# Seven products instead of eight for the convolution's output projection, a fifth early pair, and the memory values computed earlier

## The chip, the cores and the metric

The kernel runs on one core of one Trainium2 chip. The metric is the device time of one execution in microseconds (us); lower is better. The core has a matrix engine (TensorE, PE in the profile), VectorE (DVE), ScalarE (ACT), GpSimd (POOL) and SyncE (SP), whose queue issues all DMA transfers of this kernel. SBUF is the working memory, PSUM holds the sums of matrix products, and each engine works through its own list of instructions in order.

## The reference

A two-layer trunk on x of 1024 tokens by 1024 channels, with 256 memory tokens, in float32. Layer 0 mixes by attention and retention, layer 1 by a gated convolution, and each layer then adds a cross-attention into the memory. What matters here is layer 1:

```python
def conv_mixer(xn, w_in, conv_w, conv_b, w_out):
    gb, gc, u, gate = jnp.split(xn @ w_in, 4, axis=-1)
    z = gc * u
    zp = jnp.pad(z, ((0, 0), (C_CONV - 1, 0), (0, 0)))
    conv = conv_b
    for j in range(C_CONV):
        conv = conv + zp[:, j:j + s] * conv_w[j]
    y = gb * conv * jax.nn.silu(gate)
    return y @ w_out
...
x = x + conv_mixer(rmsnorm(x, o_norm[j]), ...)
x = x + memory_cross_attention(rmsnorm(x, c_norm[i]), rmsnorm(mem, c_mem_norm[i]), ...)
```

`w_in` is 1024 x 4096, `w_out` 1024 x 1024. In the cross-attention keys and values are products of the normed memory with 1024 x 1024 matrices, and queries one of the normed x.

## The kernel before, in words

**Precision.** Every large product is made from float32 data split into a high part (a copy rounded to the matmul's type, by ScalarE) and a low part (data minus high part, by VectorE): `split` (L204) for data, `Weights.whole` (L83) and `Weights.factor` (L92) for weights. `mm3` (L185) then issues three matmuls for each block of 128 x 128 weights and up to 512 columns: high x high (L189), high x low (L190), low x high (L191).

**Layout.** Activations lie channels by tokens: 8 tiles of 128 channels x 1024 tokens. `dense` (L193) makes one tile of outputs from one weight tile (128 x 1024) in two halves of 512 tokens, each of 8 blocks, 24 matmuls.

**Weights.** `Weights` takes an ordered list of weight tiles (L1065). Each is loaded by SP (L76) into one of two raw buffers, split into pages (three high buffers, three low ones) as soon as a page is free, and taken in order by the products. `prepare` (L112) works ahead as far as pages reach.

**Seven products.** `strassen` (L629) makes a pair of output tiles from 4 weight blocks (A11, A12, A21, A22; 128 outputs x 512 inputs each) and 4 activation blocks (B11 to B22; 512 channels x 512 tokens) with seven products instead of eight (Winograd's form): weights A11, A12, S1 to S4, A22 against B11, B21, T1, T2, T3, B22, T4. A product is 4 blocks x 3 = 12 matmuls. The sums S1 to S4 (L99 to L102) are made from the raw weights, by GpSimd, for the first pair by VectorE. The factors T1 to T4 are made by `right_factors` (L564) from the normed x, on VectorE, in an order fixed by `issue_after`; T2 has two buffers of its own. Before, only the convolution's input projection (`conv_in`, L707: 16 pairs, 112 products) is made like this. `times` (L670) turns products into y or z: z multiplies two of the four parts (L683 on GpSimd, L689 on VectorE), y is a gate's silu times another part.

**Early pairs.** The first two products of a pair need only B11 and B21, which come from the first half of the tokens. `conv_start` (L693) issues these two for the first EARLY = 4 pairs, so that PE has work while the norm of the second half and T1 to T4 are made.

**The stages around the change.** `out_proj_halves` (L301) is layer 0's last output projection, first half of the tokens, then the second. Between the tiles of the first half `keys_out` (L790) makes layer 1's memory keys and stores them to DRAM (24 matmuls of 256 columns per tile). Then follow `conv_start`, `conv_in`, and `out_proj` (L281), the convolution's output projection with whole products on the split y: per tile it loads the residual x (L287), adds it (L291), squares the result on ScalarE (L247), sums squares on GpSimd (L249), and stores x. Between its first four tiles `mem_v` (L823) makes the memory values (8 steps of 12 matmuls). `gained` (L915) splits the new x tiles times a gain for the queries, and `cross` (L882) follows.

**Order.** The program is traced in the order of the code, and a list scheduler with a simulated timeline sets each engine's order from readiness and program order. PSUM has 8 buffers of 512 columns: "d" 3, "sc" 2, "a" 3. SBUF buffers go by tag (L165): xh and xl 8 each, r 8, e 4, T 5, v 4, t 5.

Of the kernel before, what the change touches and what calls it, by code (L numbers as in the profile page):

```python
# [22 lines left out]
P = 128  # L23
D = 1024
# [7 lines left out]
EARLY = 4  # L32
# [8 lines left out]
class Weights:  # L41
# [5 lines left out]
    FACTORS = ("A11", "A12", "S1", "S2", "S3", "S4", "A22")  # L47
    LATER = FACTORS[2:]

    def __init__(self, tc, pool, sums, order):  # L50
# [10 lines left out]
        for _, f in self.units:  # L61
            self.tags.append(("whi", "wlo") if f is None else (("whi", "wlo")[pages % 2],))
            pages += f is not None
        self.next = 0
        self.used = 0
        self.factors = {}

    def load(self, i):
        if i >= len(self.order) or i in self.raw:
            return  # L70
        entry = self.order[i]
        tiles = []
        for k, ap in enumerate(entry[:2] if isinstance(entry, tuple) else (entry,)):
            t = self.pool.tile([P, D], F32, tag="wraw", bufs=WRAW, name=f"wraw{i}_{k}")
            for c in halves(i == 0):
                self.nc.sync.dma_start(t[:, c], ap[:, c])  # L76
            tiles.append(t)
# [14 lines left out]
    def factor(self, u, i, f):  # L92
        if f == self.order[i][2][0]:
# [9 lines left out]
            self.factors = F  # L103
        t = self.page(self.tags[u][0], f"wf{u}")
        src, hi, lo = self.factors[f], t[:, :H], t[:, H:]
# [3 lines left out]
        if f == self.order[i][2][-1]:  # L109
            self.raw.pop(i)  # L110

    def prepare(self, upto=None):  # L112

        while self.next < len(self.units) and (upto is None or self.next <= upto):
# [5 lines left out]
            self.load(i)  # L120
            if f is None:
# [7 lines left out]
    def take(self):  # L129
        u = self.used  # L130
# [5 lines left out]
class Trunk:  # L136
# [144 lines left out]
    def out_proj(self, ys, x_old, x_new, between=iter(())):  # L281
# [17 lines left out]
        return xs, old  # L299

# [263 lines left out]
    def right_factors(self, x, gain, h, out):  # L564
# [6 lines left out]
             for i in range(2) for j in range(2)}  # L571
        def normed(f):
            for k in range(4):
# [4 lines left out]
        def split(f, src):  # L578
            for k in range(4):
                if f in ("T2", "T1"):  # L580
# [3 lines left out]
                else:  # L584
                    tag = {"B11": "xh", "B21": "xh", "T3": "xl", "B22": "xl", "T4": "Tn"[k // 2]}[f]
                    t = self.buf(tag, f, dt=F32R)
# [12 lines left out]
        T2 = [t[:, i, :] for t in (self.buf("T", "T2", (P, 2, H)) for _ in range(2)) for i in range(2)]  # L599
# [23 lines left out]
        with ExitStack() as behind:  # L623
            for make in (t1, t2, t3, lambda: split("B22", B["B22"]), t4):
                last = make()
                behind.enter_context(self.tc.issue_after(last.ins))
                behind.enter_context(self.tc.issue_after(self.last_cast.ins))

    def strassen(self, B, out, early=False):  # L629
# [3 lines left out]
        def product(ps, f, first, weights=None):  # L633
            ah, al = weights or self.w.take()
            with self.tc.issue_after(self.last_mm.ins) if early == 0 and early is not False else ExitStack():
# [4 lines left out]
        def kept(ps):  # L640
            t = self.buf("t", "kept", (P, H))
            self.nc.scalar.copy(t, ps)
            return t

        a, b = self.ps("sc" if early is False or early < 2 else "d"), self.ps("d")
        if early is False:
            product(a, "B11", True)
            p1 = kept(a)
            product(b, "B21", True)
        else:  # L650
            wh, wl = self.w.take()
            product(a, "B11", True, (wh[:, :H], wl[:, :H]))
            p1 = kept(a)
            product(b, "B21", True, (wh[:, H:], wl[:, H:]))
        out(0, 0, b, p1)
        yield
# [7 lines left out]
        product(c, "B22", False)  # L664
        out(0, 1, c, u2)
        product(a, "T4", False)
        out(1, 0, a, None)
        yield

    def times(self, B, d, act=None, early=False):  # L670
# [3 lines left out]
        kept = []  # L674

        def out(i, j, ps, more):
            c = d[:, half[j]]
            if i == 0:
# [3 lines left out]
                if j:  # L682
                    nc.gpsimd.tensor_tensor(c, c, kept[0], op=ALU.mult)  # L683
# [7 lines left out]
        return self.strassen(B, out, early)  # L691

    def conv_start(self, B):  # L693
# [13 lines left out]
    def conv_in(self, B):  # L707
# [3 lines left out]
        def pair(i):  # L711
            if i < EARLY:
                d, steps = self.started[i]
            else:
                d = self.buf("v", "z" if i % 2 else "y1")
                steps = self.times(B, d, None if i % 2 else AF.Silu)
# [7 lines left out]
        for m in range(KT):  # L724
# [3 lines left out]
            nc.scalar.activation(cv, z, AF.Identity, bias=w[3], scale=w[2])  # L728
            nc.vector.scalar_tensor_tensor(cv[:, 1:], z[:, : S - 1], w[1], cv[:, 1:],
                                           ALU.mult, ALU.add)  # L730
# [347 lines left out]
```

## Time and profile before

| | |
|---|---|
| time, median of 3 runs | 1484.37 us (1483.30 to 1485.54) |
| profiled execution | 1482.23 us, its span 1480.1 us, mean clock of TensorE 0.994 |
| PE busy | 1438.2 us (97%), 7218 instructions |
| DVE / ACT / POOL busy | 878.1 / 634.8 / 322.7 us |
| conv_start and conv_in | 801.3 to 1133.4 us of the span |
| convolution's output projection | 1133.4 to about 1246 us |
| read from / written to memory | 122.80 / 25.17 MB |

Times inside the profile are microseconds from the span's start. "PE busy" counts matmuls that overlap in a pipeline, so a busy PE is not PE at its peak: the rate of matmuls in a stretch tells more. A timeline row has the start, the length, the engine, the line, the operation with output <- input, the count, and in brackets the idle time before it and what ended that. A row of waits reads: engine and line that waited, the releaser, us in total, times, longest. In the rows by stretch each engine has its busy time and (x) its instructions, followed by the clock granted to TensorE (1.00 is full), the DMA engines' busy share and GB/s.

### The profile page before, as it was taken

The numbers are of one execution on the slowest core, as the hardware profiler recorded it, in microseconds if no ns is written. First come the engines' busy times: TensorE is split into PE (matmuls) and PEld (weight loads), VectorE is DVE, ScalarE is ACT, GpSimd is POOL, SyncE is SP. The second block draws the span as 40 slices with busy tenths as digits, with TensorE's granted clock in tenths as the row PEclk, the third lists the DMA queues.
The fourth block names the chain that finished last, engine by engine and source line by source line (L and its number), as shares of the span: only waits on it lengthen the run. The fifth ranks groups of instructions, "written<-read, shape, count | busy, mean of one in ns | idle before, by whom it ended". The sixth has DMA issues, their size and how long they took to land.

```text
span 1480.1 us, 18711 instructions
## 1 busy us (share of the span) xinstructions
PE 1438.2 (97%) x7218; PEld 1215.4 (82%) x7218; DVE 878.1 (59%) x1289; ACT 634.8 (43%) x1139; POOL 322.7 (22%) x201
## 2 busy tenths in 40 slices
PE   8999999999899999999999799999999999999996
PEld 6888888888788888888888578888888888888996
DVE  7656765656674346446456967666665337446555
ACT  6434662334463344335344533333352325335554
POOL 2300103233311110000213455333340220000233
PEclk9999999999999999999999899999999999999999
DMA  6410114221365421013764121111125532111364
GB/s 216 149 65 29 58 30 142 61 79 48 119 224 170 151 92 43 29 42 129 226 201 143 42 86 58 57 57 57 58 86 213 186 128 72 39 33 40 127 210 152
DMA packets 51625, 153.38 MB, mean 104 GB/s; under 512 B 6352, under 2 KB 14672, under 8 KB 51024
## 3 DMA queue, kind: packets, MB, share of 16 engines
q1 hardware_dynamic: 51536, 152.19, 31.7%
q8 instruction: 57, 0.93, 0.3%
q14 instruction: 32, 0.26, 0.1%
HBM read 122.80 MB, written 25.17 MB: 100 GB/s over the span
## 4 chain that ended last, share of the span: by engine, by line
PE 79%; DVE 8%; DMA 5%; POOL 3%; issue 2%; ACT 2%; SPq 0%; DVEq 0%; POOLq 0%; ACTq 0%
PE psd L191 17%; PE psd L189 17%; PE psd L190 17%; PE pssc L191 5%; PE pssc L189 5%; PE pssc L190 5%; PE psa L190 4%; PE psa L189 4%; PE psa L191 4%; DMA swap<-bk 1%; PE pssc L367 1%; DMA swap<-bq 1%; PE psa L397 1%; PE psa L871 1%; POOL bk L432 1%
## 5 line engine op out<-in xcount | busy, mean ns | idle before, releaser
L189 PE MATMUL psd<-xh,whi 128*128 128x512 f32 (+2 forms) x1096 | 414.2, 381 | 7.7 <-ACT whi L87 7.3
L190 PE MATMUL psd<-xl,whi 128*128 128x512 f32 (+2 forms) x1096 | 414.7, 379 | 0.0
L191 PE MATMUL psd<-xh,wlo 128*128 128x512 f32 (+2 forms) x1096 | 414.3, 379 | 0.2 <-DVE wlo L88 0.2
L189 PEld LDWEIGHTS psd<-xh,whi 128*128 128x128 f32 x1096 | 206.4, 188 | 43.2 <-ACT whi L87 7.8
L191 PEld LDWEIGHTS psd<-xh,wlo 128*128 128x128 f32 x1096 | 206.3, 188 | 35.6 <-DVE wlo L88 0.7
L190 PEld LDWEIGHTS psd<-xl,whi 128*128 128x128 f32 x1096 | 206.5, 188 | 34.0
L87 ACT CAST whi<-wraw 128x1024 fp32r<-128x1024 f32 (+1 forms) x135 | 140.8, 1045 | 213.9 <-PE psd L190 131.0
L88 DVE TENSOR_TENSOR wlo<-wraw,whi 128x1024 fp32r<-128x1024 f32 (+1 forms) x135 | 169.1, 1254 | 71.1 <-ACT whi L87 71.0
L249 POOL TENSOR_TENSOR ssq<-ssq,xold 128x512 f32<-128x512 f32 (+2 forms) x54 | 84.6, 1567 | 574.5 <-ACT xold L247 503.0
L106 ACT CAST wf<-ws 128x512 fp32r<-128x512 f32 x64 | 39.7, 622 | 95.2 <-PE pssc L191 27.7
L291 DVE TENSOR_TENSOR xnew<-psd,xold 128x512 f32<-128x512 f32 x32 | 21.9, 690 | 96.4 <-PE psd L191 93.1
L189 PE MATMUL pssc<-T,wf 128*128 128x512 f32 x168 | 67.1, 399 | 6.6 <-ACT T L205 4.2
L190 PE MATMUL pssc<-T,wf 128*128 128x512 f32 x168 | 67.2, 400 | 1.9 <-DVE T L206 1.9
L191 PE MATMUL pssc<-T,wf 128*128 128x512 f32 x168 | 66.9, 398 | 0.0
L247 ACT ACTIVATE xold<-xnew 128x512 f32<-128x512 f32 (+2 forms) x63 | 36.5, 580 | 66.9 <-DVE xnew L291 37.1
L107 DVE TENSOR_TENSOR wf<-ws,wf 128x512 fp32r<-128x512 f32 x64 | 51.8, 811 | 20.7 <-ACT wf L106 19.6
L107 DVE TENSOR_TENSOR wf<-wraw,wf 128x512 fp32r<-128x512 f32 x40 | 55.1, 1393 | 5.0 <-ACT wf L106 5.0
L205 ACT CAST Th<-psa 128x512 fp32r<-128x512 f32 (+1 forms) x62 | 34.3, 588 | 54.2 <-PE psa L871 29.5
L206 DVE TENSOR_TENSOR Tl<-psa,Th 128x512 fp32r<-128x512 f32 (+1 forms) x62 | 41.7, 686 | 21.4 <-ACT Th L205 21.1
L278 DVE TENSOR_TENSOR q<-psd,R 128x512 f32<-128x512 f32 x32 | 22.1, 691 | 53.8 <-PE psd L191 53.8
L99 POOL TENSOR_TENSOR ws<-wraw 128x512 f32<-128x512 f32 x15 | 32.0, 2131 | 90.5 <-DMA wraw<-w_o_in 90.5
L189 PE MATMUL psd<-y,whi 128*128 128x512 f32 x128 | 50.0, 391 | 0.0
(324 smaller groups left out, 2949.4 us busy)
## 6 DMA issues: line engine op xcount, KB each, us to landing
wraw<-w_o SPq DMA_DIRECT2D x40, 512.0 KB, 4.2
wraw<-w_o_in SPq DMA_DIRECT2D x36, 512.0 KB, 3.6
wraw<-w_e_in SPq DMA_DIRECT2D x25, 512.0 KB, 3.6
wraw<-w_k SPq DMA_DIRECT2D x16, 512.0 KB, 3.9
xold<-x SPq DMA_DIRECT2D x16, 512.0 KB, 5.1
wraw<-w_v SPq DMA_DIRECT2D x16, 512.0 KB, 3.8
x<-xnew SPq DMA_DIRECT2D x16, 512.0 KB, 2.6
wraw<-w_q SPq DMA_DIRECT2D x16, 512.0 KB, 3.5
```

Of the source, the lines that this page charges most:

```text
L87: self.nc.scalar.copy(hi[:, c], raw[:, c])
L88: self.nc.vector.tensor_tensor(lo[:, c], raw[:, c], hi[:, c].bitcast(F32), op=ALU.subtract)
L99: tt(F["S1"], F["A21"], F["A22"], op=ALU.add)
L106: self.nc.scalar.copy(hi, src)
L107: self.nc.vector.tensor_tensor(lo, src, hi.bitcast(F32), op=ALU.subtract)
L189: mm(o, ah, bh, start=first, stop=False, skip_group_check=more)
L190: mm(o, ah, bl, start=False, stop=False, skip_group_check=more)
L191: self.last_mm = mm(o, al, bh, start=False, stop=last, skip_group_check=more)
L205: self.last_cast = self.nc.scalar.copy(hi, src)
L206: return (eng or self.nc.vector).tensor_tensor(lo, src, hi.bitcast(F32), op=ALU.subtract)
L247: nc.scalar.activation(sq, x, AF.Square)
L249: eng.tensor_tensor(self.ssq[:, a:b], self.ssq[:, a:b], sq, op=ALU.add)
```

## The change

- `EARLY` becomes 5, and the fifth early pair's output lies in a T buffer, its accumulator in an "a" buffer.
- The weight sums of the first pair of the input projection are an entry of their own ("sums") ahead of the early pages: its two tiles are loaded, the four sums made, and the raw buffers freed; A22 is loaded again as a half page later.
- The order of the products within a pair becomes B11, T1, B21, T2, T3, B22, T4. The last pair of each projection has the last two swapped, and the convolution's last tile is made in halves.
- T2 takes T1's place instead of two T buffers. The last multiplication of y and z moves from GpSimd to VectorE.
- The convolution's output projection becomes `out_proj_pairs`: four pairs of seven products. Its factors come from `right_factors` without gain and norm. The residual is loaded for a pair when its first product is kept, and VectorE adds it as it keeps a product (`keep`; in `times` it is a copy on ScalarE). Weight sums there are VectorE's. The squares' sums go from GpSimd to VectorE. The first product (B11) of the first OUT_EARLY = 3 pairs is issued ahead.
- Layer 1's memory values are made together with the keys between the first half's tiles of `out_proj_halves`, stored to DRAM (`values_out`) and loaded back behind the projection (`values_in`). `mem_v` is left to layer 0, and a second load of the normed memory goes.
- The first query products of `cross` use the "sc" buffers.

The core of the diff:

```diff
-EARLY = 4
+EARLY, OUT_EARLY = 5, 3
...
-    FACTORS = ("A11", "A12", "S1", "S2", "S3", "S4", "A22")
-    LATER = FACTORS[2:]
+    FACTORS = ("A11", "S1", "A12", "S2", "S3", "S4", "A22")
+    LATER = ("S1", "S2", "S3", "S4", "A22")
+    SWAPPED = ("A11", "S1", "A12", "S2", "S3", "A22", "S4")
...
+        if f == "sums":
+            self.summed = {j for j, e in enumerate(self.order)
+                           if j > i and isinstance(e, tuple) and e[0] is self.order[i][0]}
+            self.raw.pop(i)
+            return
...
+    def out_proj_pairs(self, B, x_old, x_new, early):
...
+        def pair(n):
+            old, new = [], []
+
+            def fetch():
+                for i in range(2):
+                    old.append(self.buf("v", "xold"))
+                    nc.sync.dma_start(old[i], x_old[2 * n + i])
+                new.extend(self.buf("r", "xnew") for _ in range(2))
+                xs[2 * n : 2 * n + 2] = new
+
+            def keep(i, j, ps):
+                t = self.buf("t", "kept", (P, H))
+                if not old:
+                    fetch()
+                nc.vector.tensor_tensor(t, ps, old[i][:, half[j]], op=ALU.add)
+                return t
+
+            def out(i, j, ps, more):
+                c = half[j]
+                x, sq = new[i][:, c], self.buf("t", "sq", (P, H))
+                nc.vector.tensor_tensor(x, ps, old[i][:, c] if more is None else more, op=ALU.add)
+                end = 2 * n + 2 == KT and i != j
+                self.squares(j in seen, x, sq, c.start, c.stop, None if end else nc.vector)
...
+                nc.sync.dma_start(x_new[2 * n + i][:, c], x)
+            return self.strassen(B, out, keep, None, n if n < early else False,
+                                 2 * n + 2 == KT)
+
+        started = []
+        for n in range(early):
+            started.append(pair(n))
+            next(started[n])
+        for n in range(KT // 2):
+            for _ in started[n] if n < early else pair(n):
+                pass
...
+        if gain is None:
+            tags = {"B11": "xh", "T1": "xh", "T3": "xl", "B22": "xl", "T4": "Tv"}
+            inside = ("B21", "T2")
...
-        T2 = [t[:, i, :] for t in (self.buf("T", "T2", (P, 2, H)) for _ in range(2)) for i in range(2)]
+        T2 = T1
...
-        a, b = self.ps("sc" if early is False or early < 2 else "d"), self.ps("d")
-        if early is False:
+        a = self.ps("sc" if (early or apart or 0) < 2 else "a" if early == 4 else "d")
+        if early is None:
             product(a, "B11", True)
-            p1 = kept(a)
-            product(b, "B21", True)
+            if apart is not False:
+                yield
+            p1 = keep(0, 0, a)
...
         c = self.ps("a")
         product(c, "T1", True)
-        p5 = kept(c)
+        p5 = keep(1, 1, c)
+        if early is None:
+            b = self.ps("d")
+            product(b, "B21", True)
+            out(0, 0, b, p1)
         product(a, "T2", False)
-        u2 = kept(a)
+        u2 = keep(0, 1, a)
         product(a, "T3", False)
         out(1, 1, a, p5)
...
+        for block in (c21, c12) if swapped else (c12, c21):
+            block()
...
-                    nc.gpsimd.tensor_tensor(c, c, kept[0], op=ALU.mult)
+                    nc.vector.tensor_tensor(c, c, kept[0], op=ALU.mult)
...
-                d = self.buf("v", "z" if i % 2 else "y1")
+                d = self.buf("v" if i < 4 else "T", "z" if i % 2 else "y1")
...
+    def values_out(self, mem):
+        self.vd = self.dp.tile([2, P, 2, D], F32, name="vd")
+        for ch in range(2):
+            ps = [self.ps("sc"), self.ps("sc")]
+            for kp in range(4):
+                self.value_step(mem, ps, kp)
+                if kp == 3:
+                    c = slice(ch * H, ch * H + H)
+                    for kk in range(2):
+                        hi, lo = (self.buf("t", "V", (P, H), F32R) for _ in range(2))
+                        self.split(hi, lo, ps[kk])
+                        nc.sync.dma_start(self.vd[0, :, kk, c], hi.bitcast(F32))
+                        nc.sync.dma_start(self.vd[1, :, kk, c], lo.bitcast(F32))
+                yield
...
-        self.out_proj_halves(ys, xd[0], xd[1], self.keys_out(self.mem_parts(1, "T")), after)
+        mem = self.mem_parts(1, "T")
+        both = (None for _ in zip(self.keys_out(mem), self.values_out(mem)))
+        self.out_proj_halves(ys, xd[0], xd[1], both, after)
         ys = self.conv_in(B)
...
-        ys = [self.split_k(y) for y in ys]
-        x, rest = self.out_proj(ys, xd[1], xd[2], kv)
+        B = {}
+        for h in range(2):
+            self.right_factors(ys, None, h, B)
+        x, rest = self.out_proj_pairs(B, xd[1], xd[2], OUT_EARLY)
+        K, V = self.keys_in(), self.values_in()
         xs = self.gained(x, 2)
...
+    for m, w in enumerate(tiles("w_o0")):
+        order += [w] + mem1[2 * m : 2 * m + 2]
+    order += tiles("w_o0") + [(*o_in[:2], ("sums",), True)] + o_in[: 2 * EARLY : 2]
+    order += [(*o_in[:2], W.LATER[:4]), o_in[1][:, H:]]
+    for i in range(2, len(o_in), 2):
+        last = i + 2 == len(o_in)
+        order.append((o_in[i], o_in[i + 1],
+                      W.LATER if i < 2 * EARLY else W.SWAPPED if last else W.FACTORS)
+                     + (True,) * last)
+    order += [w[:, :H] for w in o_out[: 2 * OUT_EARLY : 2]]
+    for i in range(0, len(o_out), 2):
+        last = i + 2 == len(o_out)
+        order.append((o_out[i], o_out[i + 1],
+                      (W.SWAPPED if last else W.FACTORS)[i < 2 * OUT_EARLY :], True))
```

More of the change, by code (lines that the diff above doesn't have):

```diff
@@ L60, in __init__ @@
         pages = 0
-        for _, f in self.units:
-            self.tags.append(("whi", "wlo") if f is None else (("whi", "wlo")[pages % 2],))
-            pages += f is not None
+        for i, f in self.units:
+            if f == "sums":
+                self.tags.append(())
+                continue
+            paged = f is not None or order[i].shape[-1] < D
+            self.tags.append((("whi", "wlo")[pages % 2],) if paged else ("whi", "wlo"))
+            pages += paged
         self.next = 0
@@ L74, in load @@
             t = self.pool.tile([P, D], F32, tag="wraw", bufs=WRAW, name=f"wraw{i}_{k}")
-            for c in halves(i == 0):
+            t = t[:, : ap.shape[-1]]
+            for c in halves(True) if i == 0 else (slice(0, ap.shape[-1]),):
                 self.nc.sync.dma_start(t[:, c], ap[:, c])
@@ L92, in factor @@
     def factor(self, u, i, f):
-        if f == self.order[i][2][0]:
+        if i not in self.summed and f == self.order[i][2][0]:
             a, b = self.raw[i]
@@ L108, in factor @@
         self.parts[u] = (hi, lo)
-        if f == self.order[i][2][-1]:
-            self.raw.pop(i)
     def prepare(self, upto=None):
@@ L119, in prepare @@
             i, f = self.units[u]
-            self.load(i)
-            if f is None:
+            if i not in self.summed:
+                self.load(i)
+            if f is None and len(self.tags[u]) == 1:
+                self.paged(u, self.raw.pop(i)[0])
+            elif f is None:
                 self.whole(u, i)
@@ L129, in take @@
     def take(self):
+        self.prepare()
+        while self.units[self.used][1] == "sums":
+            self.used += 1
         u = self.used
@@ L571, in right_factors @@
              for i in range(2) for j in range(2)}
+        if gain is None:
+            tags = {"B11": "xh", "T1": "xh", "T3": "xl", "B22": "xl", "T4": "Tv"}
+            inside = ("B21", "T2")
+        else:
+            tags = {"B11": "xh", "B21": "xh", "T3": "xl", "B22": "xl", "T4": "Tn"}
+            inside = ("T1", "T2")
         def normed(f):
+            if gain is None:
+                return
             for k in range(4):
@@ L584, in split @@
                 else:
-                    tag = {"B11": "xh", "B21": "xh", "T3": "xl", "B22": "xl", "T4": "Tn"[k // 2]}[f]
-                    t = self.buf(tag, f, dt=F32R)
+                    tag = tags[f]
+                    t = self.buf(tag if f != "T4" else tag[k // 2], f, dt=F32R)
                     hi, lo = t[:, :H], t[:, H:]
@@ L625, in right_factors, with strassen @@
                 last = make()
-                behind.enter_context(self.tc.issue_after(last.ins))
-                behind.enter_context(self.tc.issue_after(self.last_cast.ins))
-    def strassen(self, B, out, early=False):
+                if gain is not None:
+                    behind.enter_context(self.tc.issue_after(last.ins))
+                    behind.enter_context(self.tc.issue_after(self.last_cast.ins))
+    def strassen(self, B, out, keep, early=None, apart=False, swapped=False):
         def product(ps, f, first, weights=None):
             ah, al = weights or self.w.take()
-            with self.tc.issue_after(self.last_mm.ins) if early == 0 and early is not False else ExitStack():
+            with self.tc.issue_after(self.last_mm.ins) if early == 0 else ExitStack():
                 for k, (bh, bl) in enumerate(B[f]):
@@ L689, in out @@
                 nc.vector.tensor_tensor(c, ps, c, op=ALU.mult)
-        return self.strassen(B, out, early)
+        return self.strassen(B, out, keep, early, swapped=swapped)
     def conv_start(self, B):
```

88 lines of the change are left out of this document (56 added, 32 removed).

## The prediction

> **What bounds the kernel now.** I read the page first (busy time, then the chain that ended last), then the windows by stage, then TensorE's waits, then the timelines of the one stage that loses time.
>
> ```profile
> span 1480.1 us, 18711 instructions
> PE 1438.2 (97%) x7218; PEld 1215.4 (82%) x7218; DVE 878.1 (59%) x1289; ACT 634.8 (43%) x1139; POOL 322.7 (22%) x201
> PE 79%; DVE 8%; DMA 5%; POOL 3%; issue 2%; ACT 2%; SPq 0%; DVEq 0%; POOLq 0%; ACTq 0%
> ```
>
> TensorE (PE) is the bound: 79% of the chain is its own work. Time comes only from fewer matmuls or from the places where PE waits. The windows say where those are (columns: length, then busy time and instructions of PE, PEld, DVE, ACT, POOL, granted clock, DMA share, GB/s):
>
> ```profile
> 801.30:823.90 22.60, 22.51 (x99) 18.32 (x98) 17.60 (x27) 13.92 (x21) 0.00 (x0) 1.00 0.20 66
> 823.90:848.40 24.50, 15.81 (x49) 11.27 (x47) 24.37 (x41) 12.24 (x21) 14.20 (x2) 0.79 0.15 43
> 848.40:885.00 36.60, 34.73 (x148) 27.58 (x149) 22.30 (x25) 14.63 (x25) 19.50 (x14) 1.00 0.27 86
> 885.00:1133.40 248.40, 248.40 (x1097) 205.68 (x1096) 160.30 (x164) 91.51 (x146) 97.08 (x62) 1.00 0.24 76
> 930.00:1130.00 200.00, 200.00 (x884) 165.62 (x883) 127.52 (x131) 76.24 (x121) 72.52 (x47) 1.00 0.24 79
> 1133.40:1152.00 18.60, 18.37 (x81) 14.72 (x81) 13.17 (x13) 9.38 (x10) 0.45 (x1) 1.00 0.57 193
> 1152.00:1246.00 94.00, 94.00 (x416) 77.86 (x415) 39.40 (x44) 33.37 (x42) 18.01 (x12) 1.00 0.40 139
> ```
>
> The fifth row is the undisturbed rate: 200 us for 884 matmuls of 512 columns, 0.226 us each. A product is 12 of them (2.71 us), a pair of output tiles 7 products (19.0 us). Counted at that rate, the input projection loses nothing from 885 on (1097 x 0.226 = 248), 3.1 us in 848 to 885 (36.6 less 148 x 0.226), and 13.4 us in 823.9 to 848.4 (24.5 less 49 x 0.226). The output projection (last two rows) loses next to nothing: the memory values' products cover its start.
>
> ```profile
> PE pssc L189 <- ACT T L205: 4.2, 1, 4.2
> PE pssc L189 <- ACT kept L642: 2.4, 1, 2.4
> PE pssc L190 <- DVE T L206: 1.9, 1, 1.9
> 831.00:838.20 7.20, 5.34 (x12) 3.65 (x12) 7.20 (x13) 4.21 (x8) 4.00 (x1) 0.53 0.24 69
> 838.20:845.20 7.00, 4.62 (x13) 3.49 (x13) 7.00 (x12) 4.72 (x9) 7.00 (x1) 0.75 0.00 0
> 811.74 1.22 DVE L88 TENSOR_TENSOR wlo<-wraw,whi 128x1024 fp32r<-128x1024 f32 x1
> 842.26 2.49 DVE L620 TENSOR_TENSOR xnew<-xnew,T 128x512 f32<-128x512 f32 x4
> 847.07 1.18 DVE L206 TENSOR_TENSOR T<-xnew,T 128x512 fp32r<-128x512 f32 x1
> 834.20 13.49 POOL L99 TENSOR_TENSOR ws<-wraw 128x512 f32<-128x512 f32 x1 [34.67 <-DMA wraw<-w_o_in]
> 847.73 0.62 ACT L106 CAST wf<-ws 128x512 fp32r<-128x512 f32 x1 [2.33 <-POOL ws L99]
> ```
>
> In that stage VectorE (DVE) works without a break from 811.74 to 848.25 (36.5 us) on the right factors T1 to T4. Products follow as their factors arrive, and the next pair's weight sums stand still too: GpSimd's L99 takes 13.49 us and ends as VectorE's run does. A 128x512 operation in such a run costs a slot of 0.6 us (2.49 for four).
>
> **The change, part by part.**
>
> *Fewer products.* The output projection has 8 tiles x 2 halves x 8 blocks x 3 = 384 matmuls, and with seven products 4 pairs x 7 x 12 = 336. The 48 that go are 48 x 0.226 = **-10.9 us**. The memory values' products only move, into the first half of the projection ahead of conv_start; their number stays.
>
> *Fifth early pair.* It puts 24 matmuls (5.4 us) ahead of T1, where PE now waits for T2. VectorE's run loses four weight sums (2.4 us, now made ahead) and gains one page's low part and one addition (1.2 + 0.6), so it ends near 847.7. GpSimd still makes the sums of the second pair and still stands until then, so what PE does from 848 on stays, while 5.4 us of work has left it: 5.4 + 0.6 = **-6**. Bounds: -3 if the fifth pair waits for its page or its PSUM buffer (three "d", two held), -9 if the 3.1 us behind 848 go too. Loading the first pair's two weight tiles ahead of the early pages delays those:
>
> ```profile
> ACT whi L87 <- DMA wraw<-w_o_in: 5.8, 1, 5.8
> 794.63 1.22 DVE L88 TENSOR_TENSOR wlo<-wraw,whi 128x1024 fp32r<-128x1024 f32 x1 [3.28 <-ACT whi L87]
> ```
>
> ScalarE already waits 5.8 us for an early page, whose low part ends at 795.85, 5.5 us before its use at 801.3. One more load and four sums cost some 7 to 8 us, so PE may start 2 us late; VectorE's run, not PE, sets the end, and I cost it at nothing (bound: the 2 us).
>
> *The new transition.* This is what the change adds to the path: the output projection's own factors B11 to T4 are 28 low parts and 16 subtractions, 44 slots (26.4 us), where there were eight whole splits. The last pair of the input projection has this room:
>
> ```profile
> 1114.30:1133.40 19.10, 19.10 (x86) 15.83 (x85) 10.51 (x11) 2.59 (x3) 2.20 (x1) 1.00 0.45 174
> 1116.66 3.50 DVE L206 TENSOR_TENSOR xl<-cv,xh 128x1024 fp32r<-128x1024 f32 x3 [2.22 <-PE psa L191]
> 1120.67 4.62 DVE L206 TENSOR_TENSOR xl<-cv,xh 128x1024 fp32r<-128x1024 f32 x4
> ```
>
> VectorE is busy 10.51 us of it, 8.1 of them the splits that go, so 16.7 are free. New there: six page low parts (3.6), the first pair's sums (2.4), a multiplication from GpSimd (0.6), the convolution's half 0 (1.9): about 8 us are left for factors, and they take B11, T1 and most of B21 (15 slots, 9 us). Behind the last product's end, E: backlog 1, the convolution's second half 5 slots with one ScalarE step (3.7), 29 factor slots (17.4), and of the first pair 3 keeps, 2 outputs, 5 low parts and 4 sums (14 slots, 8.4): T4 is ready at E + 30.5 and its product ends at E + 31. PE has three early products and six more up to T4's end: 9 x 2.71 = 24.4. The shortfall is 6.7 us, or 1.3 if PE can put T1 and B21 of the second pair in between (their sums are VectorE's now and come early enough). I take **+4**, between, because the trace of before shows both: products of two pairs mixed behind 848, none of it ahead. Bounds: 0 and +9.
>
> [...] The row comes first: behind the one wait of 4.2 us the clock stood at 0.53 and 0.75, which cost 7.2 x 0.47 + 7.0 x 0.25 = 5.1 us of PE time. [...]
>
> *Keep on VectorE, sums on VectorE, squares on VectorE.* Per pair 4 sums, 7 low parts, 3 keeps, 4 outputs and 4 additions of squares are 22 slots, 13.2 us, and two gained splits:
>
> ```profile
> L218 DVE SCALAR_TENSOR_TENSOR xl<-xnew,gains,xh 128x1024 fp32r<-128x1024 f32 x16 | 20.0, 1277 | 2.3 <-ACT xh L217 2.3
> ```
>
> at 1.28 make 15.8 of 19.0 us: hidden by PE, but at 83%. The loads of x stand on SP's queue behind the buffer that they need; the first x tile of a pair is free after T2 of the pair before, so its load is covered by four products. At the end four gained splits cannot start before the last product frees their buffers (4 x 1.28 = 5.1, beside dense work on the other four blocks, 5.4): **+1** (0 to 4).
>
> *Values moved ahead.* Per tile PE now works for the projection, the keys and the values:
>
> ```profile
> 690.00:757.00 67.00, 66.89 (x388) 58.82 (x387) 31.53 (x41) 25.38 (x36) 10.47 (x6) 1.00 0.71 228
> 754.48 1.05 ACT L87 CAST whi<-wraw 128x1024 fp32r<-128x1024 f32 x1 [3.76 <-PE psd L190]
> 762.82 1.05 ACT L87 CAST whi<-wraw 128x1024 fp32r<-128x1024 f32 x1 [3.52 <-PE psd L190]
> 705.46 0.33 SPq L76 DMA_DIRECT2D wraw<-w_o  x1
> L88 DVE TENSOR_TENSOR wlo<-wraw,whi 128x1024 fp32r<-128x1024 f32 (+1 forms) x135 | 169.1, 1254 | 71.1 <-ACT whi L87 71.0
> wraw<-w_o SPq DMA_DIRECT2D x10, 512.0 KB, 4.7
> DMA to landing us min/median/max: 3.4/3.6/7.3
> ```
>
> A tile takes 8.34 us now, with the values 8.34 + 2.71 = 11.05, for three pages: 3.68 us each. A raw buffer's turn is 0.33 + 4.7 + 1.05 + 1.25 = 7.3 us, with two of them 3.67 a page. That just holds; traffic rises, so I allow landings up to 5 us, 0.15 x 24 pages: **+1.5** (0 to 5). SP also issues eight stores of values (0.33 each), among the weights' loads.
>
> The multiplications moved from GpSimd (0.6 each, 16 of them) lie in stages where PE is the bound: nothing.
>
> **The sum.** -10.9 - 6 + 4 + 1 + 1.5 = -10.4. The profiled execution took 1482.23 us (span 1480.1 and 2.1 around it) and would take 1471.8; the median of the runs is 1484.37, 2.1 above it: **1474.0**.
>
> **The rivals.**
>
> *A: the transition is covered.* PE fills the waits with the next pair's products and nothing else appears: -10.9 - 7 + 1 = -17, 1467. For: sums on VectorE come in program order. Against: VectorE's list of 30.5 us against 24.4.
>
> *B: VectorE becomes the bound of the output projection.* No filling, one long wait and the half clock behind it: 6.7 + 5.1 = 11.8 for the transition, 4 at the end: -10.9 - 6 + 11.8 + 4 + 1.5 = 0, 1484.8 at worst; with either half of it 1479. For: 83% per pair, on top of a backlog. Against: PE's seven products per pair leave VectorE 3 us each to catch up.
>
> *C: slower, by the weights' supply.* Each first-half tile needs three pages through two raw buffers. If landings take 7.3 us (the longest seen) a page takes (7.3 + 2.63) / 2 = 4.97, 1.29 more than PE allows, times 24 pages = 31; with the rest of the sum (-11.9) that is +19, 1503. It outweighs the gain from 0.5 us a page on, a landing of 5.7. For: 228 GB/s and a share of 0.71 in that stage already. Against: there ScalarE's casts wait for PE, not for loads, and three pages lie ready.
>
> **How the numbers follow.** About 0.2% (3 us) is what a measurement can tell from no change. Forecast 0.50, A 0.22, B 0.18, C 0.10. A and the forecast are faster; of B I put 0.11 beyond 3 us of gain and 0.05 within; C 0.10 slower, with 0.02 of B: faster 0.83, same 0.05, slower 0.12. The range takes in A and the unknown costs: low, -10.9 - 9 + 1 = -19, 1465; high, B's middle and beyond, 1483, which leaves out C and B's worst.
>
> **What would show it.** 48 fewer matmuls; in the stage behind conv_start no wait ahead of T2 and the loss of 16 us down to about 10, VectorE's run unchanged in length; at the input projection's end waits of PE for casts or low parts of T3, B22 and T4 that sum to about 4 us; VectorE over 80% busy behind it; PE full in the first half with values. Wrong would be: a wait for a landing in the first half (C), a clock below 1.00 at the transition (B), or an output projection without any wait (A).

## The result and the profile after

The changed kernel took 1495.67 us (median, 1493.84 to 1498.84), beside 1483.30 for the kernel before (1481.22 to 1485.54) on the same chip. The ratio is 1.0087, with a 95% interval of 1.0067 to 1.0107: **slower by 12.9 us** by this ratio, where 10.4 less were predicted. The profiled execution took 1497.8 us.

The first lines of the page after, in the order of those shown of before:

```profile
span 1495.9 us, 18739 instructions
PE 1438.1 (96%) x7170; PEld 1210.3 (81%) x7170; DVE 917.7 (61%) x1407; ACT 649.9 (43%) x1179; POOL 254.6 (17%) x169
PE 77%; DVE 12%; DMA 6%; POOL 2%; ACT 2%; issue 1%; SPq 0%; DVEq 0%; POOLq 0%; ACTq 0%
```

The 48 matmuls are gone (7218 to 7170), yet PE is as long "busy" as before (1438.1 us for 1438.2): its work has become slower in places (24.61 us for 85 matmuls from 1142.8 to 1177.2, 0.29 each, beside 0.226). VectorE's share of the chain rose from 8% to 12%. The windows of the changed kernel say where. The first is the half of layer 0's output projection that has the values, the next two are the input projection from its first early product on, and the rest is the new output projection. It is counted from the end of its own first product, with 12 matmuls of the convolution still behind that:

```profile
700.00:800.00 100.00, 100.00 (x532) 86.55 (x531) 50.69 (x61) 42.24 (x59) 9.95 (x6) 1.00 0.74 225
826.57:892.10 65.53, 56.82 (x242) 44.44 (x241) 55.93 (x78) 34.69 (x57) 16.39 (x9) 1.00 0.23 67
892.10:1142.80 250.70, 250.70 (x1107) 207.52 (x1106) 163.77 (x209) 98.22 (x166) 66.05 (x48) 1.00 0.20 60
1142.80:1177.20 34.40, 24.61 (x85) 17.74 (x84) 29.48 (x49) 14.90 (x24) 0.00 (x0) 0.80 0.31 100
1177.20:1196.40 19.20, 16.66 (x64) 12.49 (x63) 11.34 (x18) 4.99 (x8) 0.00 (x0) 0.91 0.38 125
1196.40:1219.20 22.80, 21.41 (x92) 16.71 (x92) 14.10 (x23) 11.88 (x17) 0.00 (x0) 1.00 0.45 148
1219.20:1246.50 27.30, 22.63 (x90) 17.57 (x89) 18.51 (x25) 9.05 (x12) 0.00 (x0) 0.94 0.85 291
```

Count each row at the undisturbed rate of 0.226 us a matmul. The first half with the values (first row) is full. The stage behind the first early product loses 65.5 - 242 x 0.226 = 10.8 us, where before lost 16.7. The rest of the input projection loses nothing. The output projection, which lost nothing before, now loses 15.2 us at its start (34.4 - 85 x 0.226) and 4.7, 2.0 and 6.9 in the three stretches behind it.

TensorE's waits in the start, 1142.8 to 1177.2:

```profile
PE psd L213 <- ACT B L229: 3.3, 1, 3.3
PE psd L214 <- DVE B L230: 2.4, 1, 2.4
PE psa L215 <- DVE wf L127: 2.3, 1, 2.3
PE pssc L213 <- DVE second L782: 1.5, 1, 1.5
```

These name splits and pages as late. What was missing, though, is something else to do meanwhile, and the timelines of VectorE, SP and TensorE show why. The third fence is a row of SP's waits.

```profile
1153.38 0.68 DVE L785 TENSOR_TENSOR z<-pssc,z 128x512 f32<-128x512 f32 x1
...
1171.69 0.68 DVE L347 TENSOR_TENSOR kept<-pssc,xold 128x512 f32<-128x512 f32 x1
```

```profile
1146.51 12.24 SPq L86 DMA_DIRECT2D wraw<-w_o_out  x3
1159.75 1.53 SPq L339 DMA_DIRECT2D xold<-x  x2
```

```profile
SPq L339 <- DVE cv L829: 1.0, 1, 1.0
```

```profile
1142.58 0.39 PE L215 MATMUL pssc<-B,wf 128*128 128x512 f32 x1
...
1157.90 0.39 PE L215 MATMUL psa<-T,wf 128*128 128x512 f32 x1
1161.63 0.58 PE L213 MATMUL psd<-B,wf 128*128 128x512 f32 x1 [3.34 <-ACT B L229]
...
1171.04 0.63 PE L214 MATMUL psa<-T,wf 128*128 128x512 f32 x1
...
1177.27 0.39 PE L213 MATMUL pssc<-T,wf 128*128 128x512 f32 x1
```

The first pair's first product ends with the first matmul shown, at 1142.58, in an "sc" buffer. It is kept (L347, which adds x) only at 1171.69, and T2, which accumulates into the same buffer, starts only at 1177.27. The load of x that the keep needs was issued at 1159.75, when the convolution's multiply-adds (L829) had read the last z: its v buffers were those of the convolution's last y and z. SP waited only 1.0 us for that read, because its list, too, has the load late, behind three weight loads. The first tile landed 4.4 us after its issue, at about 1164. VectorE's list has the keep later still, behind the splits of B21 and others: VectorE worked without a break from 1150.4 and came to it 7.5 us after the landing. Until then PE had the three early products, T1 and most of B21, used them up by 1157.90, and went idle.

### The profile page after: what moved, and what is told of

It is laid out like the page before. It is cut to its first block, busy times and chain, and to the rows that moved or that the text cites. A ratio compares the mean times of both kernels' runs of the same rounds, so it can differ in the third digit from the quotient of the medians.

```text
span 1495.9 us, 18739 instructions
## 1 busy us (share of the span) xinstructions
PE 1438.1 (96%) x7170; PEld 1210.3 (81%) x7170; DVE 917.7 (61%) x1407; ACT 649.9 (43%) x1179; POOL 254.6 (17%) x169
## 4 chain that ended last, share of the span: by engine, by line
PE 77%; DVE 12%; DMA 6%; POOL 2%; ACT 2%; issue 1%; SPq 0%; DVEq 0%; POOLq 0%; ACTq 0%
PE psd L213 14%; PE psd L215 14%; PE psd L214 14%; PE pssc L215 6%; PE pssc L214 6%; PE pssc L213 6%; PE psa L215 4%; PE psa L214 4%; PE psa L213 4%; DVE T L230 1%; DMA swap<-bk 1%; PE pssc L439 1%; DVE wf L127 1%; DMA swap<-bq 1%; PE psa L469 1%
## 5 line engine op out<-in xcount | busy, mean ns | idle before, releaser
L213 PE MATMUL psd<-xh,whi 128*128 128x512 f32 (+2 forms) x936 | 353.8, 380 | 8.3 <-ACT whi L97 7.0
L214 PE MATMUL psd<-xl,whi 128*128 128x512 f32 (+2 forms) x936 | 352.9, 378 | 0.0
L215 PE MATMUL psd<-xh,wlo 128*128 128x512 f32 (+2 forms) x936 | 352.7, 378 | 0.0
L213 PEld LDWEIGHTS psd<-xh,whi 128*128 128x128 f32 x936 | 176.2, 188 | 38.3 <-ACT whi L97 7.6
L215 PEld LDWEIGHTS psd<-xh,wlo 128*128 128x128 f32 x936 | 176.4, 188 | 28.7
L214 PEld LDWEIGHTS psd<-xl,whi 128*128 128x128 f32 x936 | 176.6, 189 | 27.9
L213 PE MATMUL pssc<-T,wf 128*128 128x512 f32 x192 | 75.1, 391 | 4.9 <-ACT kept L769 2.6
L214 PE MATMUL pssc<-T,wf 128*128 128x512 f32 x192 | 74.9, 390 | 0.2 <-DVE T L230 0.2
L215 PE MATMUL pssc<-T,wf 128*128 128x512 f32 x192 | 74.6, 389 | 0.0
L126 ACT CAST wf<-wraw 128x512 fp32r<-128x512 f32 x50 | 31.0, 621 | 50.1 <-PE pssc L215 44.0
L213 PE MATMUL psd<-y,whi 128*128 128x512 f32 x128 | 49.9, 390 | 0.0
L214 PE MATMUL psd<-y,whi 128*128 128x512 f32 x128 | 49.9, 390 | 0.0
L215 PE MATMUL psd<-y,wlo 128*128 128x512 f32 x128 | 49.8, 389 | 0.0
```

What stands on the lines that cost most here:

```text
L126: self.nc.scalar.copy(hi, src)
L213: mm(o, ah, bh, start=first, stop=False, skip_group_check=more)
L214: mm(o, ah, bl, start=False, stop=False, skip_group_check=more)
L215: self.last_mm = mm(o, al, bh, start=False, stop=last, skip_group_check=more)
```

## The experiments

Kernels of one batch ran on one chip beside the kernel before, so ratios to it are compared. A difference of ratios of 0.001 is 1.5 us. The loss of the output projection is read from one stretch that all profiles share, 1142 to 1246: its 104 us less 0.226 for each matmul. It is that of the one profiled execution, which can lie off the kernel's median (e4_no_residual's by 5 us below, g3_first_gp's by 5 us above), so it is read beside the ratio. Before and after:

```profile
1142.00:1246.00 104.00, 104.00 (x460) 85.99 (x459) 44.28 (x50) 37.06 (x47) 18.46 (x12) 1.00 0.42 145
```

```profile
1142.00:1246.00 104.00, 85.62 (x328) 64.75 (x327) 73.72 (x114) 40.32 (x61) 0.00 (x0) 0.90 0.49 164
```

Nothing (460 matmuls) and 29.8 us (328). All runs in one table:

| kernel | median us | ratio to before, 95% interval | loss there, us |
|---|---|---|---|
| the change | 1495.67 | 1.0087 (1.0067 to 1.0107) | 29.8 |
| e1_early_only | 1482.06 | 0.9982 (0.9972 to 0.9991) | 0 |
| e2_gp_sums | 1498.43 | 1.0092 (1.0076 to 1.0107) | 28.0 |
| e3_x_ahead | 1494.90 | 1.0068 (1.0053 to 1.0083) | 25.5 |
| e4_no_residual | 1481.70 | 0.9973 (0.9963 to 0.9982) | 10.6 |
| f1_ve_keep | 1481.36 | 0.9982 (0.9973 to 0.9992) | 12.8 |
| f2_gp_resid | 1483.19 | 0.9994 (0.9980 to 1.0007) | 16.2 |
| f3_gp_resid_x | 1483.11 | 0.9993 (0.9982 to 1.0005) | 14.9 |
| f4_none_early | 1495.93 | 1.0093 (1.0067 to 1.0119) | 26.6 |
| g1_x0_slot | 1488.52 | 1.0024 (1.0015 to 1.0033) | 18.3 |
| g2_t4_behind | 1484.60 | 1.0001 (0.9988 to 1.0014) | 16.0 |
| g3_first_gp | 1487.20 | 1.0014 (1.0003 to 1.0025) | 21.9 |
| g4_rest_gp | 1489.52 | 1.0046 (1.0029 to 1.0062) | 20.5 |
| h1_behind_x | 1482.47 | 0.9988 (0.9979 to 0.9998) | 13.7 |
| h2_behind_gp | 1481.12 | 0.9977 (0.9964 to 0.9990) | 10.1 |
| h3_behind_gpsums | 1484.76 | 1.0002 (0.9991 to 1.0014) | 14.4 |
| h4_behind_none | 1485.71 | 1.0012 (1.0002 to 1.0021) | 16.5 |

### First batch: which part is it?

The letters are those of the expectations: V, VectorE's list is made too long by the weight sums; R, the loads of x come late; C, the way in which the convolution ends; X, the early pairs bring what was predicted of them, and Y, they don't.

**e1_early_only**: the input projection's part alone; the output projection and the values as before.

```diff
-        self.out_proj_halves(ys, xd[0], xd[1], both, after)
+        self.out_proj_halves(ys, xd[0], xd[1], self.keys_out(self.mem_parts(1, "T")), after)
...
-        x, rest = self.out_proj_pairs(B, xd[1], xd[2], OUT_EARLY)
+        x, rest = self.out_proj(ys, xd[1], xd[2], kv)
```

> The fifth early pair, the sums ahead and the new order of products alone; output projection, values and their cover as before. Theory X (all of the loss lies in the new output projection): 1483 - 6 = 1477 us, with the loss of TensorE behind conv_start about 10 us and none at the output projection. Theory Y (the early pair's gain is given back later, or layer 0 is slower with it): 1481 or more.

Measured 0.9982, a gain of 2.7 us (1.3 to 4.2). The sign of X, the size of Y. The stage itself gained less here than in the changed kernel: in the 94.2 us behind the first early product the loss is 16.8 us before (342 matmuls), 13.0 in e1_early_only (359) and 10.9 in the changed kernel (368). No run shows why. The rest of the change, then, costs some 16 us where the prediction had it gain 4.

**e2_gp_sums**: the output projection's weight sums back on GpSimd.

```diff
-                      (W.SWAPPED if last else W.FACTORS)[i < 2 * OUT_EARLY :], True))
+                      (W.SWAPPED if last else W.FACTORS)[i < 2 * OUT_EARLY :]))
```

> As the changed kernel, but the output projection's weight sums on GpSimd again. Theory V (VectorE's list: its sums stand, waiting for weight loads, ahead of the convolution's last outputs and of the keeps): 6 to 10 us faster than 1495.7, so 1486 to 1490. Theory R (the residual tiles arrive late) and theory C (the cover of the values' products is gone): no change within 2 us, or slower by GpSimd's longer sums.

1.0092, no gain: V falls in that form. Sixteen sums fewer in VectorE's list change nothing while something else is late.

**e3_x_ahead**: three of T4's tiles in T buffers, so that one more v buffer is free for x.

```diff
-            tags = {"B11": "xh", "T1": "xh", "T3": "xl", "B22": "xl", "T4": "Tv"}
+            tags = {"B11": "xh", "T1": "xh", "T3": "xl", "B22": "xl", "T4": "TTTv"}
...
-                    t = self.buf(tag if f != "T4" else tag[k // 2], f, dt=F32R)
+                    t = self.buf(tag if f != "T4" else tag[k], f, dt=F32R)
```

> As the changed kernel, but three of T4's four tiles lie in T buffers, so that three v buffers are left for the residual tiles instead of two and both tiles of the next pair can be loaded before the pair begins. Theory R: the waits at the three pair boundaries (13.6 us of lost TensorE time) go for the most part, 8 to 12 us faster: 1484 to 1488. Theories V and C: 1494 to 1497, as the changed kernel.

1.0068, a gain of 2.8 us by point estimates whose intervals overlap; the time lies where V and C had it. The changed kernel's wait at the last pair (first fence) is gone from e3_x_ahead, but the start still waits as it did (second fence):

```profile
PE psa L213 <- DVE kept L347: 2.8, 1, 2.8
```

```profile
PE psd L213 <- ACT B L229: 3.6, 1, 3.6
PE psd L214 <- DVE B L230: 2.5, 1, 2.5
```

So R holds for that one wait, and not for the 12 us. In the first pair the loads were not issued earlier (first at 1162.4 us, in a trace that lies some 3 us later there).

**e4_no_residual**: x neither loaded nor added.

```diff
-                    nc.sync.dma_start(old[i], x_old[2 * n + i])
...
-                nc.vector.tensor_tensor(t, ps, old[i][:, half[j]], op=ALU.add)
+                nc.scalar.copy(t, ps)
```

> As the changed kernel with the residual left out of the output projection: x is neither loaded nor added there, a kept product is a copy on ScalarE. Theory R: 10 to 14 us faster, 1482 to 1486, with the loss left at the transition (15 us). Theory V: some 4 us faster from 12 VectorE operations less, 1491. Theory C: no change beyond 2 us.

0.9973, 17 us under the changed kernel: the residual costs more than the 10 to 14 us that R had put at, and C falls as the account of the slowdown, though the stage still loses 10.6 us without x. Open is whether it is VectorE that keeps, or x that it waits for.

### Second batch: the keeping, or the wait?

**f1_ve_keep**: as e4_no_residual, but VectorE copies.

```diff
-                nc.scalar.copy(t, ps)
+                nc.vector.tensor_copy(t, ps)
```

> The changed kernel with no residual, as in e4_no_residual, but the kept products of the output projection are copied out of PSUM by VectorE, which adds x there in the changed kernel (the residual is left out of the output). Theory L (the wait for the transfers of x is what costs): nothing waits for a transfer here, so it stays at the time without residual, 1480 to 1484. Theory K (it is the keeping itself: it stands in VectorE's list behind splits, sums and lower halves, and holds PSUM until VectorE comes to it): most of the 14 us between e4_no_residual and the changed kernel come back, 1490 to 1496.

0.9982, and 12.8 us of loss where the changed kernel has 29.8:

```profile
1142.00:1246.00 104.00, 96.30 (x403) 75.62 (x402) 82.70 (x126) 43.15 (x66) 0.00 (x0) 0.98 0.44 142
```

VectorE works more here than in the changed kernel (82.7 us of 104, beside 73.7), and the stage is 17 us better. Theory K falls as to the work of keeping, and L holds: without x the same engine makes the first keep at 1150.65, ahead of the convolution's last z, and with x at 1171.69. Of that delay the 7.5 us behind the landing are VectorE's list, as K has it; but the order of that list is different once x is late (the scheduler sets it by readiness; that this alone moved the keep is argued, not tested).

**f2_gp_resid** and **f3_gp_resid_x**: whole kernels. ScalarE copies the kept product out of PSUM, and GpSimd adds x to the copy; f3_gp_resid_x has the buffers of e3_x_ahead too.

```diff
-                nc.vector.tensor_tensor(t, ps, old[i][:, half[j]], op=ALU.add)
+                nc.scalar.copy(t, ps)
+                nc.gpsimd.tensor_tensor(t, t, old[i][:, half[j]], op=ALU.add)
```

> The changed kernel, whole: ScalarE copies the kept products out of PSUM as before in the convolution, and GpSimd then adds x to the copy in place, three adds for each pair. Theory K: PSUM is free without VectorE or x, 1482 to 1488. Theory L: the transfers are waited for as before, now by the add ahead of the first output of a pair, 1489 to 1495.

> f2_gp_resid with T4 in the T buffers but for its last tile, so that three v buffers are free for x and its loads are issued a product or more earlier. Theory L: 1482 to 1487, clearly under f2_gp_resid. Theory K: within 3 us of f2_gp_resid.

0.9994 and 0.9993. x is loaded as late as before (first at 1159.9), but the wait no longer holds PSUM, nor VectorE's list: 13.8 us come back. That is where theory K had both; L had expected the late x to cost as much wherever it is added, and in this it was wrong. The buffers of f3_gp_resid_x add nothing (first load at 1158.3). Together with f1_ve_keep: the price is the late x **at the place where it frees a PSUM buffer**. Late x alone (f2_gp_resid, 16.2 us of loss there) and a keep by VectorE alone (f1_ve_keep, 12.8) are each cheap beside the 29.8 of both.

**f4_none_early**: OUT_EARLY = 0.

```diff
-EARLY, OUT_EARLY = 5, 3
+EARLY, OUT_EARLY = 5, 0
```

> The changed kernel with none of the output projection's products ahead of the last convolution's end (three in the changed kernel). If the three products cover the conv and the splits behind it, as the prediction has it, TensorE waits some 8 us longer there: 1500 to 1505. If they are spent before the wait comes and what follows is bound by VectorE's list anyway, 1494 to 1498.

1.0093, as the changed kernel: as long as the keep is late, the three early products buy nothing that can be measured.

### Third batch: the first pair, or the later ones?

**g1_x0_slot**: the first pair's x in T buffers.

```diff
-                    old.append(self.buf("v", "xold"))
+                    old.append(self.buf("v" if n else "T", "xold"))
```

> The changed kernel with the first pair's two tiles of x in T buffers, which are free then, in place of v buffers, which the convolution's last z and y hold; the loads stand where they stood, at the first keep. If it is the v buffers that hold the first loads back, they are issued some 10 us earlier and most of the 13 us come back: 1483 to 1488. If SP's queue holds them too (the weight loads ahead of them wait for pages of VectorE's), or VectorE's list has the keep late anyway: 1492 to 1497.

1.0024, 9.3 us under the changed kernel: the larger part of the gain. Its first load and its first keep:

```profile
1150.72 0.33 SPq L339 DMA_DIRECT2D xold<-x  x1
```

```profile
1157.79 0.68 DVE L347 TENSOR_TENSOR kept<-pssc,xold 128x512 f32<-128x512 f32 x1
```

9 and 14 us earlier. With a free buffer the first load also stands ahead of two of the weight loads in SP's list, so the buffers did hold it back. The second tile's load stayed at 1159.76.

**g2_t4_behind**: T4 is formed behind the first keep in VectorE's list, and takes its v buffers after x.

```diff
-                nc.vector.tensor_tensor(t, ps, old[i][:, half[j]], op=ALU.add)
+                add = nc.vector.tensor_tensor(t, ps, old[i][:, half[j]], op=ALU.add)
+                if self.late:
+                    with self.tc.issue_after(add.ins):
+                        self.late.pop()()
...
+                if gain is None and make is t4:
+                    self.late = [t4]
+                    break
```

> The changed kernel with T4 of the output projection formed and split behind the first pair's first keep in VectorE's list, and its two v buffers taken after x's, so that x of the first pair gets the v buffers that come free first. Theory S (the cost lies at the first pair, whose first keep comes late and holds the PSUM bank that T2 needs): the keep comes 8 us or more earlier, 1483 to 1489. Theory B (it lies at the later pairs, where x is loaded only as the pair before ends): 1493 to 1497.

1.0001, 12.8 us under the changed kernel. Its first loads, first keep, and stage:

```profile
1119.09 2.08 SPq L339 DMA_DIRECT2D xold<-x  x2
```

```profile
1144.39 0.69 DVE L347 TENSOR_TENSOR kept<-pssc,xold 128x512 f32<-128x512 f32 x1
```

```profile
1142.00:1246.00 104.00, 93.29 (x389) 72.84 (x388) 78.87 (x120) 41.79 (x63) 0.00 (x0) 0.98 0.50 164
```

The keep now comes 27 us earlier, by VectorE, with x. The edit changes two things at once, the order of the allocations and T4's place in VectorE's list; of the two, g1_x0_slot has the buffer alone (9.3 us), and T4's place alone was not run.

**g3_first_gp** and **g4_rest_gp**: f2_gp_resid's edit for the first pair alone (n == 0), and for pairs 1 to 3 alone (n > 0).

> The changed kernel with ScalarE's copy and GpSimd's add of x for the first pair's kept products alone; pairs 1 to 3 keep by VectorE. Theory S: nearly all that f2_gp_resid gained, 1483 to 1487. Theory B: 1492 to 1496.

> The reverse of g3_first_gp: the first pair keeps by VectorE, pairs 1 to 3 by ScalarE and GpSimd. Theory S: 1491 to 1496. Theory B: 1484 to 1488.

1.0014 and 1.0046: 10.8 and 6.1 us under the changed kernel, together more than f2_gp_resid's 13.8. Theory S has the larger part, but B isn't nothing: the later pairs are worth some 3 to 6 us (e3_x_ahead 2.8, by intervals that overlap; g4_rest_gp 6.1, between the ranges of both theories).

### Fourth batch: what is left

**h1_behind_x** is g2_t4_behind with e3_x_ahead's buffers; **h2_behind_gp** is g2_t4_behind with f2_gp_resid's keep in pairs 1 to 3; **h3_behind_gpsums** and **h4_behind_none** are h1_behind_x with the edit of e2_gp_sums, and with OUT_EARLY = 0.

> g2_t4_behind with the T4 buffers of e3_x_ahead, so that three v buffers stay for x in the later pairs. If the later pairs' wait for x (2.9 us of the trace of g2_t4_behind, at the last pair) ends the stage's remaining loss in part, 1480.5 to 1482.5. If something else comes last there too, 1484 to 1486.

> g2_t4_behind with ScalarE's copy and GpSimd's add of x in pairs 1 to 3. The same wait taken away in another way, and three keeps of each pair off VectorE: 1480 to 1482 if the wait for x or VectorE's share is what is left of the loss; 1484 to 1486 if neither is.

> h1_behind_x with the output projection's weight sums on GpSimd. If VectorE's sums hold back its list at the start once the wait for x is gone, 2 to 4 us under h1_behind_x. If the sums by GpSimd come later than VectorE would have made them, so that pages come late, 1 to 4 us over it. Within 1 us if neither.

> h1_behind_x with no product of the output projection ahead of the convolution's end. The prediction had these three products, 8.1 us of TensorE's work, as the cover of the last conv: without the wait that masked it in f4_none_early they should now be missed, 4 to 9 us over h1_behind_x. If they cover nothing, within 2 us of it.

h1_behind_x 0.9988 and h2_behind_gp 0.9977: 2 and 3.5 us under g2_t4_behind, by point estimates whose intervals overlap. h2_behind_gp is the fastest kernel here that computes all, 3.4 us (1.5 to 5.3) under before, beside 2.7 for e1_early_only: the two can't be told apart. Its stage still loses 10.1 us:

```profile
1142.00:1246.00 104.00, 97.14 (x415) 76.58 (x414) 87.35 (x119) 49.34 (x79) 13.56 (x9) 1.00 0.52 174
```

With GpSimd's sums the time is about 2 us longer by point estimates whose intervals overlap (h3_behind_gpsums, 1.0002 beside 0.9988): nothing speaks for moving them off VectorE. Without early products it is 3.6 us longer (1.0012 beside 0.9988, intervals apart): once the keep is in time the cover is real, though less than the 4 to 9 expected, and less than the three products' own 8.1 us.

## Why the prediction was wrong

By its own terms, in us of the profiled execution:

| term | predicted | measured |
|---|---|---|
| 48 matmuls fewer | -10.9 | -10.9 (7170 for 7218) |
| fifth early pair | -6 | -5.9 (16.7 to 10.8) |
| start of the output projection | +4 (0 to +9) | +15.2 |
| its pairs and end | +1 (0 to +4) | +13.6 |
| values ahead | +1.5 (0 to +5) | 0 |
| elsewhere: layer 0 | none | +3.5 |

The last row is the first early product's start, 826.57 for 801.30, less the 96 matmuls of the values that went ahead of it. The sum is +15.5, and the spans differ by 15.8.

**Right.** The matmuls; the early stage, to 0.1 us in this kernel, with the waits that stood among its bounds, here of the changed kernel from 826.57 to 892.1:

```profile
PE pssc L213 <- ACT kept L769: 2.6, 1, 2.6
PE psd L213 <- DVE z L775: 2.0, 1, 2.0
PE psa L215 <- DVE wf L127: 1.4, 2, 0.9
```

None waits for T2 any more. The second is the PSUM buffer that the fifth pair had to wait for, a case for which the prediction had put -3. That the stage came out at -5.9 all the same is in part luck: the same pair brought some 4 us in e1_early_only. The values ahead cost nothing: 700 to 800 is full at 225 GB/s, so rival C, which had the one mechanism for a clearly slower kernel, did not happen. (Its term in the sum was a slip: 0.15 x 24 is 3.6, not 1.5.) The kernel became slower by another.

**The step that failed** is the cover: "the first x tile of a pair is free after T2 of the pair before, so its load is covered by four products", and "PE has three early products and six more up to T4's end". The first holds for a pair that has a pair before it. The first pair has none: what stands in its v buffers is the convolution's last z and y, in use until the conv's end, and its x was issued at 1159.75, some 6 us after VectorE had made z from the convolution's last product at 1153.38. Its keep came at 1171.69. The second sentence counts T2 and what follows as cover, and T2 needs that keep. The keep is not work that may come late, for the product's PSUM buffer is what T2 and T3 accumulate in. So of the "six more" products T1 and B21 were left. The prediction counted what VectorE's list and PE's products sum to, and took from the buffers only the fifth pair's and the later pairs' x; it never followed the first keep back to its load and the load back to its buffer. The runs show each link: without the wait (f1_ve_keep), with the wait off PSUM (f2_gp_resid), with other buffers (g1_x0_slot) and with the order turned (g2_t4_behind), 9 to 16 us come back; less work for VectorE with T2 as late (e2_gp_sums, where it starts 36.4 us behind the last matmul of the first product, beside 34.7 in the changed kernel) brings none.

T2 of the first pair started at 1177.27 in the changed kernel, 23.9 us after z at 1153.38. In f1_ve_keep z comes 3.6 us later, at 1156.95, and T2 5.9 us after it:

```profile
1162.81 0.39 PE L213 MATMUL pssc<-T,wf 128*128 128x512 f32 x1
```

Up to 1157.90 PE has T1 and most of B21 to work on, which go into other PSUM buffers than the first product; the buffer that T2 needs is emptied only at 1171.69, behind a transfer.

Rival B had the lower clock (0.80), though behind several waits and not one long one, but not the cause. The forecast's +4 has no cost of a lower clock in it; no run shows how long a wait has to be for one, and here the clock fell behind waits of 3.3 and 2.4 us. The amount of VectorE's work did not bound the stage: f1_ve_keep keeps it busier and is 17 us better there. What VectorE did add is order, the 7.5 us between the landing of x and its keep. B's worst case, 1484.8, was passed by 11 us.

**The size that was off.** The pairs and their end, +1 in the sum, measured +13.6. By the medians some 3 to 6 us of the loss are the later pairs' x. With no late x on TensorE's path the start and the pairs still lose some 10 us (h2_behind_gp 10.1, e4_no_residual 10.6, f1_ve_keep 12.8), where the prediction had 5. In h2_behind_gp the waits are of 1.1 us and less, for casts, low parts, keeps and outputs, places where a product needs a page or a buffer that the engines have only just come to. A share of 83% summed over a pair does not see them. I have not taken them apart, and their cause stays open.

**Open** is layer 0. Behind a long wait there the clock fell in the changed kernel's profile and not in that of before (0.66 and 1.00 from 400 to 410, last section), in work that the change doesn't touch. That is not the whole +3.5: the first matmul behind the wait starts at 401.69 for 399.73, so 2.0 us of it stood already as the wait ended. e1_early_only, which leaves the values where they were, lies late there too: the first output of layer 0's first output projection comes at 455.1 us in the profile of before, at 458.5 in the changed kernel's and at 459.5 in that of e1_early_only. The medians differ by 12.4 us, the two profiled executions by 15.6, so the profiled executions lie on opposite sides of their medians, and not all of the +3.5 is the change's. With one profile of before, no more can be said.

## What to carry to other kernels

Where an epilogue reads something loaded while it frees a PSUM buffer, the load can lie on TensorE's path, as it did here (13.8 us came back in f2_gp_resid, where ScalarE copies the product out and GpSimd adds x): follow the first such read back to its load, and the load back to whoever holds its buffer, above all at the seam between two stages, where the steady state's argument ("the pair before has freed it") doesn't hold. Allocate the tile that is waited for first ahead of tiles that are needed later; here that, together with forming the later tile behind the first keep, was worth 13 us, and other buffers for the first tile alone 9. Work put ahead as cover was worth nothing here while what follows it was blocked: the same three products were worth nothing measurable (f4_none_early 1.0093 beside 1.0087) and, with the keep in time, 3.6 us (h4_behind_none 1.0012 beside 0.9988).

## What the runs showed of the hardware that was not expected

How long PE waited did not decide whether its clock fell. Around the bk step of layer 0 each of three profiles has one long wait. It is shown with the stretch behind it (400 to 410 us), first for before, then for the changed kernel, then for e4_no_residual:

```profile
399.73 0.63 PE L451 MATMUL psa<-ident,bk 128*128 128x128 f32 x4 [3.53 <-DVE bk L434]
```

```profile
400.00:410.00 10.00, 9.24 (x66) 7.98 (x65) 9.72 (x16) 5.89 (x13) 5.09 (x4) 1.00 0.73 254
```

```profile
401.69 1.09 PE L523 MATMUL psa<-ident,bk 128*128 128x128 f32 x4 [3.74 <-DVE bk L506]
```

```profile
400.00:410.00 10.00, 8.30 (x44) 7.81 (x45) 10.00 (x13) 6.38 (x12) 4.37 (x4) 0.66 0.67 202
```

```profile
398.77 0.63 PE L524 MATMUL psa<-ident,bk 128*128 128x128 f32 x4 [2.10 <-DVE bk L507]
```

```profile
400.00:410.00 10.00, 9.95 (x64) 9.02 (x64) 8.73 (x14) 4.92 (x12) 5.37 (x4) 0.84 0.71 216
```

A wait of 3.53 us left the clock at 1.00, one of 3.74 us went with 0.66, and one of 2.10 us with 0.84. In six more profiles the clock of this stretch lies between 0.66 and 0.83: 0.68 in e1_early_only, 0.66 in e3_x_ahead, f1_ve_keep and h2_behind_gp, 0.83 in f2_gp_resid and g2_t4_behind. The wait at this step was 3.71 us in e1_early_only, 3.43 in h2_behind_gp and 3.21 in g2_t4_behind. So the clock stayed full behind a wait longer than three of those with a lower one; what decides it no run shows. At the start of the output projection the clock fell too: behind waits of 3.3 and 2.4 us the matmuls of the changed kernel took 0.63 us at 1171.04, beside 0.39 at 1157.90. In h2_behind_gp, with no wait there above 1.1 us, the stage has 1.00.
